# One matmul for two key branches: shared scores in the second attention of a hybrid decoder layer, with its scaling moved forward and its dense work paced lower

## The chip, the cores and the metric

The kernel runs on one core of a Trainium2 chip. The metric is the device time of one execution in microseconds. TensorE (PE) multiplies, VectorE (DVE), ScalarE (ACT) and GpSimd (POOL) do the elementwise work, and SyncE (SP) issues the loads.

## The reference

One decoder layer over 512 tokens of width 1024, in float32. A normed input is projected into the columns of four token mixers; their outputs, each multiplied by a SiLU gate path, are projected, gated and added up. Two mixers are attentions of 8 heads of 64:

```python
y_a = fox_attention(rms_norm(heads(qa, FOX_HEADS), qn_a), rms_norm(heads(ka, FOX_HEADS), kn_a),
                    heads(va, FOX_HEADS), fa + b_forget)          # first attention, with decay
...
y_c = nsa_attention(rms_norm(heads(qc, NSA_HEADS), qn_c), ...)    # second attention
# in it, for each block of 128 queries:
k_sel = ks_blk[b_ix, g_ix, top_idx]                               # "selected" keys, branch s
s_s = jnp.einsum('bqgrd,bgqkld->bgrqkl', q_i, k_sel) * scale
s_w = jnp.einsum('bqgrd,bkgd->bgrqk', q_i, k_wi) * scale          # "window" keys, branch w
return g[:, :, 0] * o_c + g[:, :, 1] * o_s + g[:, :, 2] * o_w     # and compressed keys, o_c
```

With 512 tokens the selection of 16 blocks of 64 takes all 8 blocks that there are and the window covers all 512 positions, so branches s and w are both causal attentions of the same queries, over different keys and values.

## The kernel before

Every float32 matrix is split into a high part and a rest (`h`, `l` in names), and products are sums of matmuls over the parts. **Dense work** is the projections `z_...`: blocks of 24 matmuls of 128x512 (`zgen`, `chunks`), whose weights are loaded (`r_...`), and split by ScalarE or GpSimd (high) and VectorE (rest) into `w_...`.

**Attention** goes by units (class `Unit`): in the first a head is a unit (`a0` to `a7`), in the second a head is two units (`s0`, `w0`, and so on to `w7`). For a unit `scores` runs over the four blocks of 128 queries, from 3 down to 0: block i has (i + 1) x 128 causal keys. Two matmuls (`ka`, `kb`: parts of the keys) go to one of two score banks `s_...`; VectorE reads the bank with the mask and writes probabilities' arguments `p_...` with a row extreme into `nm_...`; ScalarE takes the exponential; after block 0 GpSimd scales the rows (`p_...<-p_...,nm_...`). `finish` then transposes the probabilities through banks `tb`, splits them into `ph` and `pl`, and multiplies with the values (`o_...`). `attend` writes the scores of the next unit ahead of `finish` of the one before.

`fill(us)` writes that much dense work between attention steps. Its amount per step is `G` = 0.68 us times a pace, `FOX` for the first attention and `NSA` for the second. Generators in `side` advance with dense steps.

`nsa_scales` finishes the norm of the second attention's queries `zq_c` and keys `zkm`: small VectorE steps on `tsc`, then eight GpSimd multiplies. It is called between the attentions. `k_operand` and `q_operand` then transpose and split keys (`kt_...`) and queries (`qt_...`).

Order: from the first projections to the end of the second attention the writing order is only a priority. A planner (class `Order`) records instructions with what they need, and a list scheduler with assumed costs picks for each engine the earliest written one that is ready. Behind the second attention come the recurrence's gates (`g`), merges and the output, from which later instructions may be drawn ahead.

Of the kernel before, what the change touches and what calls it, by code (L numbers as in the profile page):

```python
# [10 lines left out]
F32 = mybir.dt.float32  # L11
# [6 lines left out]
P = 128  # L18
# [48 lines left out]
class Order:  # L67
# [72 lines left out]
    def plan(self):  # L140
# [106 lines left out]
def tile_hybrid_layer(ctx: ExitStack, tc: tile.TileContext, x, xT, units, small, bsp, out):  # L247
# [9 lines left out]
    def behind(op):  # L257
        return order.behind(op) if order.on else tc.issue_after(op)
# [299 lines left out]
    ssa = cp.tile([P, 4, 16], F32, name="ssa")  # L558
    tsa = cp.tile([P, 2, 64], F32, name="tsa")
# [123 lines left out]
    xbt = pool("xbp", xbs).tile([P, 4, S], F32, name="xb")  # L683
# [22 lines left out]
    def k_operand(z, c0, gcol, kt, name):  # L706
        ka, kb = kt
        t_ = heads(z, c0, "kt_" + name)
        g = cc[:, gcol:gcol + 1]
        for e in range(2):  # L710
            r, o = HALF[e], HALF[1 - e]
            ACT.activation(ka[r, e, :], t_[r, :], AF.Identity, scale=g[r, :])
            DVE.scalar_tensor_tensor(kb[r, e, :], t_[r, :], g[r, :], f32(ka[r, e, :]), op0=ALU.mult, op1=ALU.subtract)
            POOL.tensor_scalar(ka[o, e, :], f32(ka[r, e, :]), 1.0, 0.0, op0=ALU.mult, op1=ALU.add)

    def k_tiles(pl_, name):
        ka = pl_.tile([P, 2, S], F32R, name="ka_" + name)
        kb = pl_.tile([P, 2, S], F32R, name="kb_" + name)
        for e in range(2):
            POOL.memset(f32(kb[HALF[1 - e], e, :]), 0.0)  # L720
# [12 lines left out]
    def scores(u, gap):
        u.p = p = ap.tile([P, 1280], F32, tag="p", bufs=2, name="p_" + u.name)
        nm = ap.tile([P, 12], F32, tag="nm", bufs=4, name="nm_" + u.name)
        for i in (3, 2, 1, 0):
            n = (i + 1) * P
            s = sbank(f"s_{u.name}{i}")
            qs = u.q[:, i * P:(i + 1) * P]
            PE.matmul(s[:, :n], lhsT=qs, rhs=u.ka[:, :n], start=True, stop=False)  # L740
            PE.matmul(s[:, :n], lhsT=u.q2[:, i * P:(i + 1) * P], rhs=u.kb[:, :n], start=False, stop=True)
            pi = p[:, OFF[i]:OFF[i] + n]
            DVE.tensor_tensor_reduce(out=pi, in0=s[:, :n], in1=maskm[:, 384 - i * P:512], scale=-1.0, scalar=BIG,
                                     op0=ALU.add, op1=ALU.min, accum_out=nm[:, i:i + 1])
            ACT.activation(pi, pi, AF.Exp, scale=-1.0, bias=nm[:, i:i + 1], accum_out=nm[:, 4 + i:5 + i])
            fill(gap)
        r = nm[:, 8:12]
        DVE.reciprocal(r, nm[:, 4:8])
        if u.gate is not None:
            DVE.tensor_tensor(r, r, u.gate, op=ALU.mult)  # L750
        for i in range(4):
            pi = p[:, OFF[i]:OFF[i] + (i + 1) * P]
            POOL.tensor_scalar(pi, pi, nm[:, 8 + i:9 + i], 0.0, op0=ALU.mult, op1=ALU.add)
# [4 lines left out]
    def transposes(u, g_):  # L758
# [4 lines left out]
        for c, (j, i) in enumerate(PIECES[g_]):  # L763
            PE.transpose(t_[:, c * P:(c + 1) * P], u.p[:, OFF[i] + j * P:OFF[i] + (j + 1) * P], identf)
# [84 lines left out]
    nb = kts[0][1][0:40, 1, :]  # L849
    ACT.copy(nb[0:8, :], negc)  # L850
    DVE.tensor_tensor(nb[32:40, :], negc, f32(nb[0:8, :]), op=ALU.subtract)
    ACT.copy(kts[0][1][64:104, 0, :], f32(nb))
    for e, o in ((0, 64), (1, 0)):
        POOL.tensor_scalar(kts[1][1][o:o + 40, e, :], f32(nb), 1.0, 0.0, op0=ALU.mult, op1=ALU.add)
    later(*chunks("kv", xh, xl, emit_kv), *chunks("qc", xh, xl, emit_z(zq_c, ssc, 4, 8, ap)),
# [22 lines left out]
    def fox_units():  # L878
# [8 lines left out]
        for i in range(4):  # L887
            kt, q = kts[i % 2], nxt[i]
            for e in range(2):
# [42 lines left out]
    NSA = 1.1  # L932
    FOX = 1.2
# [182 lines left out]
    kts = [k_tiles(rp2, nm) for nm in "sw"]  # L1116
    nsa_scales()
# [13 lines left out]
    k_operand(zk_c, 0, KNC, kts[0], "s")  # L1131
# [4 lines left out]
    ws = []  # L1136

# [30 lines left out]
    def second_keys():  # L1168
        k_operand(zk_c, P, KNC, kts[1], "w")
        fill(4 * G)  # L1170

    def nsa_units():
        q = q0
        for i in range(4):
# [3 lines left out]
            for n in range(4):  # L1178
                e, b = n // 2, n % 2
                h = i + 4 * e  # L1180
                if n == 1:
                    while not ready:
# [3 lines left out]
                ka, kb = kts[b]  # L1186
                yield Unit(f"{'sw'[b]}{h}", q[:, e, :], ka[:, e, :], kb[:, e, :], v_c, 2 * b + e,
                           gate=gates[:, :, 8 * (b + 1) + h], first=b == 0, last=b == 1,
                           acc=add_cmp(cell, e) if b else None, then=second_keys if i == n == 0 else None,
                           done=lambda o, h=h: evict(o, y["c"][:, h // 2, :], h % 2, f"c{h}"))  # L1190
# [572 lines left out]
```

## Time and profile before

| | |
|---|---|
| median of 3 runs | 712.65 us (712.14 to 713.6) |
| profiled execution | 713.0 us, of which the span is 711.3 |
| busy | PE 98%, DVE 80%, ACT 51%, POOL 24% |
| matmuls | 3357 |
| first attention | about 78 to 201 us from the span's start |
| second attention | about 223 to 382 us |

A row of single instructions gives its start, its duration, the engine, the operation, out<-in and shape, and in brackets the idle time before it with what ended that. A matmul's duration runs from its start to its modelled end, and the next one starts well before that: the distance from start to start is what a matmul costs. Rows of stages give the stretch, and for each engine busy time and instructions.

### The profile page before, as it was taken

How to read it: one execution, taken by the hardware profiler on the slowest of the kernel's cores; microseconds unless marked ns; L12 is line 12 of the kernel's file. 1: busy time of each engine (PE TensorE's matmuls, PEld its weight loads, DVE VectorE, ACT ScalarE, POOL GpSimd, SP SyncE). 2: the span in 40 equal slices, each digit the busy share in tenths (PEclk: the TensorE clock that was granted, in tenths of full speed). 3: DMA queues.
4: the chain of work that ended last, by engine and by line, in shares of the span. 5: the costliest groups of instructions: out<-in, count | busy, mean ns of one | idle time of the engine just before them, and what ended most of it. 6: DMA issues, size and time to landing. Idle time of an engine off the chain costs nothing.

```text
span 711.3 us, 9561 instructions
## 1 busy us (share of the span) xinstructions
PE 700.0 (98%) x3357; PEld 573.4 (81%) x3357; DVE 571.0 (80%) x1090; ACT 362.3 (51%) x677; POOL 171.2 (24%) x230
## 2 busy tenths in 40 slices
PE   8999999999999999999999999999999999999997
PEld 6888778887877888888777888888888888888876
DVE  5799676677389949889897879999778858958995
ACT  4552555675524237776566881434534551653641
POOL 4124652453346303333244312100000000000000
PEclk9999999999999999999999999999999999999999
DMA  8613132111113431100201232333522333133302
GB/s 312 240 59 119 39 110 90 60 60 62 58 60 127 141 118 60 59 31 4 87 29 60 83 110 80 102 126 138 178 93 85 113 125 112 36 119 119 118 30 88
DMA packets 20640, 68.35 MB, mean 96 GB/s; under 512 B 2416, under 2 KB 2800, under 8 KB 20592
## 3 DMA queue, kind: packets, MB, share of 16 engines
q1 hardware_dynamic: 20160, 67.25, 28.4%
q8 instruction: 26, 0.43, 0.2%
q10 hardware_dynamic: 432, 0.49, 0.2%
q14 instruction: 22, 0.18, 0.1%
HBM read 65.64 MB, written 2.10 MB: 95 GB/s over the span
## 4 chain that ended last, share of the span: by engine, by line
PE 78%; DVE 13%; issue 3%; ACT 3%; DMA 2%; POOL 2%; SPq 0%; DVEq 0%; POOLq 0%; ACTq 0%
PE pj L223 9%; PE z_mg L223 6%; PE tb L211 3%; PE z_qc L211 3%; PE z_ud L211 3%; PE z_gb L223 3%; PE z_qa L211 3%; PE z_va L211 3%; PE o_s L211 3%; PE mg2y L223 2%; PE z_vd L211 2%; PE mg1y L223 2%; PE z_xb L211 2%; PE z_ka L211 2%; PE z_kv L211 2%
## 5 line engine op out<-in xcount | busy, mean ns | idle before, releaser
L223 PE MATMUL pj<-w_wb,yh 128*128 128x512 f32 x256 | 79.8, 389 | 0.0
L223 PEld LDWEIGHTS pj<-w_wb,yh 128*128 128x128 f32 x256 | 48.1, 188 | 9.9
L223 PE MATMUL pj<-w_wb,yl 128*128 128x512 f32 x128 | 49.8, 389 | 0.0
L223 DVE TENSOR_TENSOR w_wb<-r_wb,w_wb 128x512 fp32r<-128x512 f32 x32 | 20.9, 686 | 9.5 <-ACT w_wb L223 8.5
L223 PEld LDWEIGHTS pj<-w_wb,yl 128*128 128x128 f32 x128 | 24.0, 188 | 4.9
L211 POOL TENSOR_SCALAR p_w<-p_w,nm_w 128x128 f32<-128x128 f32 (+3 forms) x32 | 16.8, 543 | 39.2 <-DVE nm_w L211 39.2
L211 DVE TENSOR_TENSOR pl_a<-tb,ph_a 128x512 fp32r<-128x512 f32 (+1 forms) x24 | 14.4, 598 | 14.2 <-ACT ph_a L211 14.0
L211 ACT CAST ph_a<-tb 128x512 fp32r<-128x512 f32 (+1 forms) x24 | 12.4, 517 | 23.3 <-PE tb L211 23.1
L211 PE MATMUL z_xb<-xh,w_xb 128*128 128x512 f32 x64 | 24.0, 409 | 0.0
L211 ACT ACTIVATE p_s<-p_s,nm_s 128x512 f32<-128x512 f32 (+3 forms) x32 | 17.8, 559 | 11.8 <-DVE nm_s L211 11.1
L211 PE MATMUL z_gd<-xh,w_gd 128*128 128x512 f32 x64 | 22.7, 403 | 0.9 <-DVE w_gd L211 0.8
L211 ACT ACTIVATE p_w<-p_w,nm_w 128x512 f32<-128x512 f32 (+3 forms) x32 | 17.9, 561 | 10.2 <-DVE nm_w L211 10.1
L211 POOL TENSOR_SCALAR p_a<-p_a,nm_a 128x128 f32<-128x128 f32 (+3 forms) x32 | 19.7, 633 | 12.7 <-DVE nm_a L211 12.0
L211 PE MATMUL z_ud<-xh,w_ud 128*128 128x512 f32 x64 | 22.6, 400 | 0.0
L211 POOL TENSOR_SCALAR p_s<-p_s,nm_s 128x128 f32<-128x128 f32 (+3 forms) x32 | 17.3, 560 | 21.3 <-ACT ph_w L211 8.0
L211 ACT ACTIVATE p_a<-p_a,nm_a 128x512 f32<-128x512 f32 (+3 forms) x32 | 17.9, 560 | 7.0 <-DVE nm_a L211 6.9
L211 PE MATMUL z_ga<-xh,w_ga 128*128 128x512 f32 x64 | 21.3, 398 | 0.0
L211 DVE CUSTOM_DVE_ANT_0 p_a<-s_a,maskm 128x512 f32<-128x512 f32 (+3 forms) x32 | 15.3, 486 | 7.4 <-PE s_a L211 4.0
L223 PE MATMUL z_gb<-xh,w_gb 128*128 128x512 f32 x64 | 21.1, 390 | 0.0
L223 ACT CAST w_wb<-r_wb 128x1024 fp32r<-128x1024 f32 x12 | 12.6, 1047 | 15.5 <-issue 15.5
L211 DVE CUSTOM_DVE_ANT_0 p_s<-s_s,maskm 128x512 f32<-128x512 f32 (+3 forms) x32 | 15.0, 485 | 4.3 <-PE s_s L211 3.8
L211 DVE TENSOR_TENSOR pl_w<-tb,ph_w 128x512 fp32r<-128x512 f32 (+1 forms) x24 | 14.0, 598 | 3.0 <-ACT ph_w L211 2.8
(812 smaller groups left out, 2323.8 us busy)
## 6 DMA issues: line engine op xcount, KB each, us to landing
r_wb<-in_units_dram SPq DMA_DIRECT2D x16, 512.0 KB, 3.7
xt<-in_x_dram SPq DMA_DIRECT2D x4, 512.0 KB, 8.4
r_ga<-in_units_dram SPq DMA_DIRECT2D x4, 512.0 KB, 3.7
r_gd<-in_units_dram SPq DMA_DIRECT2D x4, 512.0 KB, 3.9
r_ud<-in_units_dram SPq DMA_DIRECT2D x4, 512.0 KB, 4.2
r_gc<-in_units_dram SPq DMA_DIRECT2D x4, 512.0 KB, 3.7
r_xb<-in_units_dram SPq DMA_DIRECT2D x4, 512.0 KB, 3.8
r_gb<-in_units_dram SPq DMA_DIRECT2D x4, 512.0 KB, 3.8
```

Source lines behind the costliest of these rows:

```text
L211: getattr(self.eng[name], method)(*args, **kw)
L223: return lambda *args, **kw: real(*args, **kw).ins
```

## The change

1. In the second attention a head's two units are made together (`twin`). Both branches' keys lie in one tile with a branch index. For query blocks 3 and 2 each unit has its own matmuls as before. For blocks 1 and 0 the unit `s` issues one matmul whose moving operand is the keys of both branches (2 x 256 and 2 x 128 columns); VectorE and ScalarE then work on the two halves of the bank apart. The probabilities are in two tiles: `p0_...` (blocks 0 and 1, three buffers) and `p_...` (blocks 2 and 3, two). The second branch's keys are made inside the first unit (`amid`), not after it.
2. `nsa_scales` becomes a side generator, started when the last block of the `qc` projection is out, in the first attention.
3. Paces: `FOX` 1.2 to 0.6, `NSA` 1.1 to 0.5. A window unit, which has only two steps left, fills twice at each.
4. The first attention's decay operand `q2` gets four slots in a buffer that it shares with the later convolution input `xb`; two small tiles move to another pool. The planner finds the users of a buffer's former tile when it plans, no longer when it records.

```diff
-                need.update((m, True) for m, *_ in self.seen.get(self.before[t], ()))
+            for t in ops[i][6]:
+                need.update((m, True) for m, *_ in self.seen.get(self.before.get(t), ()))
...
+    q2s = xbp.tile([P, 4, S], F32R, tag="xb", bufs=1, name="q2s")
...
+    def start(u):
+        u.low = ap.tile([P, 384], F32, tag="p0", bufs=3, name="p0_" + u.name)
+        u.nm = ap.tile([P, 12], F32, tag="nm", bufs=4, name="nm_" + u.name)
...
     def scores(u, gap):
-        u.p = p = ap.tile([P, 1280], F32, tag="p", bufs=2, name="p_" + u.name)
+        both = [u, u.twin] if u.twin else [u]
+        for x in both:
+            if x.low is None:
+                start(x)
+        u.high = ap.tile([P, 896], F32, tag="p", bufs=2, name="p_" + u.name)
         for i in (3, 2, 1, 0):
-            n = (i + 1) * P
+            if i < 2 and len(both) == 1 and u.gate is not None:
+                continue
+            us = both if i < 2 else [u]
+            n, m = (i + 1) * P, (i + 1) * P * len(us)
             s = sbank(f"s_{u.name}{i}")
-            PE.matmul(s[:, :n], lhsT=qs, rhs=u.ka[:, :n], start=True, stop=False)
-            PE.matmul(s[:, :n], lhsT=u.q2[:, i * P:(i + 1) * P], rhs=u.kb[:, :n], start=False, stop=True)
+            k = (slice(None), slice(0, 2) if len(us) > 1 else u.ka[1], slice(0, n))
+            PE.matmul(s[:, :m], lhsT=u.q[:, i * P:(i + 1) * P], rhs=u.ka[0][k], start=True, stop=False)
+            PE.matmul(s[:, :m], lhsT=u.q2[:, i * P:(i + 1) * P], rhs=u.kb[0][k], start=False, stop=True)
+            for c, x in enumerate(us):
...
-            fill(gap)
+            fill(gap * (2 if u.gate is not None and len(both) == 1 else 1))
...
         rsqrt(ssc, y_, tsc[:, 1, :].rearrange("p (t h) -> p t h", t=4))
+        yield 0.0
...
+    def last_qc(t, ps):
+        emit_qc(t, ps)
+        if t == 3:
+            side.append(nsa_scales())
...
-    NSA = 1.1
-    FOX = 1.2
+    NSA = 0.5
+    FOX = 0.6
...
-    kts = [k_tiles(rp2, nm) for nm in "sw"]
-    nsa_scales()
+    kts = k_tiles(rp2, "c", 2)
```

What stands where, before and after. First TensorE at the low query blocks of the selected unit of the second pair of units (`s_s` its score bank, `tb` and `o_s` the transposes and values of the unit ahead, `z_...` dense work). Before:

```order
L211 MATMUL z_gc_2104<-xh,w_gc_2103 128x512
L211 MATMUL s_s_2017<-ka_s,q_c_1936 128x256
L211 MATMUL s_s_2017<-kb_s,q_c_1936 128x256
L211 MATMUL z_gc_2104<-xl,w_gc_2103 128x512
L211 MATMUL z_gc_2104<-xh,w_gc_2103 128x512 x2
L211 MATMUL z_gc_2104<-xl,w_gc_2103 128x512
L211 MATMUL z_gc_2104<-xh,w_gc_2103 128x512
L211 MATMUL s_s_2018<-ka_s,q_c_1936 128x128
L211 MATMUL s_s_2018<-kb_s,q_c_1936 128x128
L211 MATMUL tb_1907<-identf,p_w_1998 128x128 x2
```

After (`ka_c` and `kb_c` hold both branches):

```order
L211 MATMUL tb_79<-identf,p_w_1905 128x128 x2
L211 MATMUL z_ud_1977<-xl,w_ud_1965 128x512
L211 MATMUL s_s_1987<-ka_c,q_c_1895 128x512
L211 MATMUL s_s_1987<-kb_c,q_c_1895 128x512
L211 MATMUL s_s_1988<-ka_c,q_c_1895 128x256
L211 MATMUL s_s_1988<-kb_c,q_c_1895 128x256
L211 MATMUL z_ud_1977<-xh,w_ud_1965 128x512 x2
L211 MATMUL z_ud_1977<-xl,w_ud_1965 128x512
```

Before, blocks 1 and 0 of this unit have 256 and 128 columns, and the window unit has another such four matmuls some 30 and 40 rows on; now 512 and 256 columns serve both units, and the window unit's four are gone.

Next GpSimd at the scaling (`zkm`, `zq_c`; `p_a` are the first attention's probabilities, `ka_s` keys of the second, `w_...` weights being split). Before:

```order
L211 MEMSET kcn 64x128
L211 MEMSET hsk 64x128
L211 TENSOR_TENSOR zkm<-zkm,tsc 128x256
L211 TENSOR_TENSOR zq_c<-zq_c,tsc 128x512
L211 TENSOR_TENSOR zkm<-zkm,tsc 128x256
L211 TENSOR_TENSOR zq_c<-zq_c,tsc 128x512
L211 TENSOR_TENSOR zkm<-zkm,tsc 128x256
L211 TENSOR_TENSOR zq_c<-zq_c,tsc 128x512
L211 TENSOR_TENSOR zkm<-zkm,tsc 128x256
L211 TENSOR_TENSOR zq_c<-zq_c,tsc 128x512
L211 TENSOR_SCALAR w_gd_1955<-r_gd_1954 128x1024
L211 TENSOR_SCALAR ka_s<-ka_s 64x512 x2
```

After:

```order
L211 TENSOR_SCALAR w_vd.01_917<-r_vd.01_916 128x1024
L211 TENSOR_TENSOR zkm<-zkm,tsc 128x256
L211 TENSOR_TENSOR zq_c<-zq_c,tsc 128x512
L211 TENSOR_TENSOR zkm<-zkm,tsc 128x256
L211 TENSOR_TENSOR zq_c<-zq_c,tsc 128x512
L211 TENSOR_TENSOR zkm<-zkm,tsc 128x256
L211 TENSOR_SCALAR p_a_887<-p_a_887,nm_a_888 128x128
L211 TENSOR_SCALAR p_a_887<-p_a_887,nm_a_888 128x256
L211 TENSOR_SCALAR p_a_889<-p_a_889,nm_a_888 128x384
L211 TENSOR_SCALAR p_a_889<-p_a_889,nm_a_888 128x512
L211 TENSOR_TENSOR zq_c<-zq_c,tsc 128x512
L211 TENSOR_TENSOR zkm<-zkm,tsc 128x256
```

Before, the eight multiplies stand between the attentions, ahead of the second attention's first keys; now five stand ahead of the last head's scaling of the first attention, and three behind it.

Last TensorE where the first attention ends (`o_a` its values, `z_ga` the gate projection, `z_vd` a projection of another mixer). Before:

```order
L211 MATMUL o_a_924<-ph_a_931,v_a 128x256
L211 MATMUL o_a_924<-pl_a_932,v_a 128x256
L211 MATMUL z_ga_928<-xh,w_ga_921 128x512
L211 MATMUL z_ga_928<-xl,w_ga_921 128x512
L211 MATMUL z_ga_928<-xh,w_ga_921 128x512 x2
L211 MATMUL z_ga_928<-xl,w_ga_921 128x512
L211 MATMUL z_ga_928<-xh,w_ga_921 128x512 x2
L211 MATMUL z_ga_928<-xl,w_ga_921 128x512
L211 MATMUL z_ga_928<-xh,w_ga_921 128x512
L211 MATMUL z_ga_1930<-xh,w_ga_1929 128x512
```

After:

```order
L211 MATMUL o_a_905<-ph_a_910,v_a 128x256
L211 MATMUL z_vd_914<-w_vd.01_917,xl 128x512
L211 MATMUL o_a_905<-pl_a_911,v_a 128x256
L211 MATMUL z_vd_914<-w_vd.01_917,xh 128x512
L211 MATMUL z_vd_915<-w_vd.01_917,xh 128x512
L211 MATMUL z_vd_915<-w_vd.01_917,xl 128x512
L211 MATMUL z_vd_915<-w_vd.01_917,xh 128x512 x2
L211 MATMUL z_vd_915<-w_vd.01_917,xl 128x512
L211 MATMUL z_vd_915<-w_vd.01_917,xh 128x512
L211 MATMUL z_vd_912<-w_vd.10_920,xh 128x512
L211 MATMUL z_vd_912<-w_vd.10_920,xl 128x512
L211 MATMUL z_vd_912<-w_vd.10_920,xh 128x512 x2
```

Before, the gate projection stands there and the other projection is done; now that projection's last blocks of 48 matmuls (`w_vd.10`, `w_vd.11`) follow with nothing of an attention between them. In the same way the convolution's projection `z_xb` ended ahead of the scores of the seventh of the eight pairs of units, and now ends beside the transposes of the eighth; from the third to the sixth pair dense rows are about as few in the one order as in the other.

More of the change, by code (lines that the diff above doesn't have):

```diff
@@ L257, in behind @@
     def behind(op):
-        return order.behind(op) if order.on else tc.issue_after(op)
+        if order.on:
+            return order.behind(op)
+        return nullcontext() if isinstance(op, int) else tc.issue_after(op)
     def shut(stack):
@@ L711, in k_operand @@
             r, o = HALF[e], HALF[1 - e]
[L712 to L720, printed above, removed]
+            ACT.activation(ka[r, e, b, :], t_[r, :], AF.Identity, scale=g[r, :])
@@ new lines, in k_operand, with k_tiles @@
+            DVE.scalar_tensor_tensor(kb[r, e, b, :], t_[r, :], g[r, :], f32(ka[r, e, b, :]), op0=ALU.mult, op1=ALU.subtract)
+            POOL.tensor_scalar(ka[o, e, b, :], f32(ka[r, e, b, :]), 1.0, 0.0, op0=ALU.mult, op1=ALU.add)
+    def k_tiles(pl_, name, nb=1):
+        ka = pl_.tile([P, 2, nb, S], F32R, name="ka_" + name)
+        kb = pl_.tile([P, 2, nb, S], F32R, name="kb_" + name)
+        for b in range(nb):
+            for e in range(2):
+                POOL.memset(f32(kb[HALF[1 - e], e, b, :]), 0.0)
@@ new lines, in scores @@
+            PE.matmul(s[:, :m], lhsT=u.q[:, i * P:(i + 1) * P], rhs=u.ka[0][k], start=True, stop=False)
+            PE.matmul(s[:, :m], lhsT=u.q2[:, i * P:(i + 1) * P], rhs=u.kb[0][k], start=False, stop=True)
+            for c, x in enumerate(us):
+                pi, nm = x.row(i), x.nm
+                DVE.tensor_tensor_reduce(out=pi, in0=s[:, c * n:(c + 1) * n], in1=maskm[:, 384 - i * P:512], scale=-1.0,
+                                         scalar=BIG, op0=ALU.add, op1=ALU.min, accum_out=nm[:, i:i + 1])
+                ACT.activation(pi, pi, AF.Exp, scale=-1.0, bias=nm[:, i:i + 1], accum_out=nm[:, 4 + i:5 + i])
@@ L749, in scores @@
+            fill(gap * (2 if u.gate is not None and len(both) == 1 else 1))
+            if u.amid and i == 3:
+                u.amid()
+        r = u.nm[:, 8:12]
+        DVE.reciprocal(r, u.nm[:, 4:8])
         if u.gate is not None:
@@ L763, in transposes @@
         for c, (j, i) in enumerate(PIECES[g_]):
-            PE.transpose(t_[:, c * P:(c + 1) * P], u.p[:, OFF[i] + j * P:OFF[i] + (j + 1) * P], identf)
+            PE.transpose(t_[:, c * P:(c + 1) * P], u.row(i)[:, j * P:(j + 1) * P], identf)
         ph, pl_ = (ap.tile([P, S], F32R, tag=w, bufs=3, name=f"{w}_{u.name}{g_}") for w in ("ph", "pl"))
@@ L848, in tile_hybrid_layer @@
     kts = [k_tiles(kp, f"a{b}") for b in range(2)]
[L849 removed]
+    nb = kts[0][1][0:40, 1, 0, :]
     ACT.copy(nb[0:8, :], negc)
     DVE.tensor_tensor(nb[32:40, :], negc, f32(nb[0:8, :]), op=ALU.subtract)
[L852 removed]
+    ACT.copy(kts[0][1][64:104, 0, 0, :], f32(nb))
     for e, o in ((0, 64), (1, 0)):
[L854 to L855 removed]
+        POOL.tensor_scalar(kts[1][1][o:o + 40, e, 0, :], f32(nb), 1.0, 0.0, op0=ALU.mult, op1=ALU.add)
+    emit_qc = emit_z(zq_c, ssc, 4, 8, ap)
+    def last_qc(t, ps):
+        emit_qc(t, ps)
+        if t == 3:
+            side.append(nsa_scales())
+    later(*chunks("kv", xh, xl, emit_kv), *chunks("qc", xh, xl, last_qc),
           zgen("cm0", 0, cm_use(0)), zgen("cm0", 1, cm_use(1)))
@@ L1136, in tile_hybrid_layer @@
     ws = []
+    xbt = xbp.tile([P, 4, S], F32, tag="xb", bufs=1, name="xb")
     def conv(i, ps):
@@ L1185, in nsa_units @@
                     fill(G)
[L1186 to L1190, printed above, removed]
+                if b == 0:
+                    pair = [Unit(f"{'sw'[j]}{h}", q[:, e, :], (kts[0][:, e], j), (kts[1][:, e], j), v_c, 2 * j + e,
+                                 gate=gates[:, :, 8 * (j + 1) + h], first=j == 0, last=j == 1,
+                                 acc=add_cmp(cell, e) if j else None, amid=second_keys if i == n == j == 0 else None,
+                                 done=lambda o, h=h: evict(o, y["c"][:, h // 2, :], h % 2, f"c{h}")) for j in range(2)]
+                    pair[0].twin = pair[1]
+                yield pair[b]
                 if n == 1:
```

37 lines of the change are left out of this document (15 added, 22 removed).

## The prediction

> **What bounds the kernel now.** I read the page's busy times first, then the chain of work that ended last, then busy times by stage, then single matmuls.
>
> ```profile
> span 711.3 us, 9561 instructions
> PE 700.0 (98%) x3357; PEld 573.4 (81%) x3357; DVE 571.0 (80%) x1090; ACT 362.3 (51%) x677; POOL 171.2 (24%) x230
> PEclk9999999999999999999999999999999999999999
> PE 78%; DVE 13%; issue 3%; ACT 3%; DMA 2%; POOL 2%; SPq 0%; DVEq 0%; POOLq 0%; ACTq 0%
> 549.84 5.44 PE mg1z L223 x24
> ```
>
> TensorE is the bound: in use for 98% of the span at full granted clock, with 78% of the chain. The last row, from the chain, gives the price of a full matmul with nothing in its way: 5.44/24 = 0.227 us from start to start (128x512). Gains come from fewer matmuls, or from the time that TensorE loses between them. I call that time slack: over all matmuls of a stage, the distance from one start to the next, less the price of that shape. The other prices:
>
> ```profile
> 288.16 0.28 PE L211 MATMUL s_s<-ka_s,q_c 128*128 128x256 f32 x1
> 288.27 0.28 PE L211 MATMUL s_s<-kb_s,q_c 128*128 128x256 f32 x1
> 288.39 0.63 PE L211 MATMUL z_gc<-xh,w_gc 128*128 128x512 f32 x2
> 289.19 0.22 PE L211 MATMUL s_s<-ka_s,q_c 128*128 128x128 f32 x1
> 289.25 0.28 PE L211 MATMUL s_s<-kb_s,q_c 128*128 128x128 f32 x1
> 289.37 0.65 PE L211 MATMUL tb<-identf,p_w 128*128 128x128 f32 x4
> 309.27 0.34 PE L211 MATMUL s_w<-ka_w,q_c 128*128 128x384 f32 x1
> 309.44 0.28 PE L211 MATMUL o_s<-pl_w,v_c 128*128 128x256 f32 x1
> 229.07 0.60 PE L211 MATMUL kt_w<-identf,zkm 128*128 128x128 f32 x4
> 229.43 0.71 PE L211 MATMUL z_gd<-xh,w_gd 128*128 128x512 f32 x2
> 229.97 0.39 PE L211 MATMUL z_gd<-xl,w_gd 128*128 128x512 f32 x1
> ```
>
> By starts: a pair of 256 columns 0.23, a pair of 128 columns 0.18, one of 384 0.17; four transposes with the delay of what follows 0.90 - 2 x 0.227 = 0.45. With these (0.227, 0.175, 0.119, 0.085, and 0.109 a transpose) I summed the slack by stage, for the matmuls counted in the PE column:
>
> ```profile
> core 0: us, PE busy (x) PEld busy (x) DVE busy (x) ACT busy (x) POOL busy (x), PEclk, DMA share, GB/s
> 84.00:200.00 116.00, 115.27 (x590) 95.60 (x590) 78.41 (x165) 66.42 (x147) 49.50 (x72) 1.00 0.23 73
> 200.00:226.00 26.00, 24.31 (x112) 18.54 (x111) 23.88 (x42) 7.36 (x11) 16.97 (x17) 1.00 0.31 101
> 226.00:262.00 36.00, 35.82 (x178) 29.39 (x178) 25.85 (x72) 13.22 (x32) 7.51 (x10) 1.00 0.41 132
> 262.00:383.00 121.00, 120.04 (x689) 100.01 (x688) 104.53 (x301) 79.57 (x210) 42.21 (x70) 1.00 0.15 49
> 383.00:395.00 12.00, 11.83 (x51) 8.95 (x50) 11.97 (x17) 8.83 (x14) 5.26 (x6) 1.00 0.26 79
> ```
>
> Slack: first attention (84 to 200) 3.9 us; change of attention (200 to 226) 3.6; compression (226 to 262) 0.9; second attention (262 to 383) 9.1; recurrence gates (383 to 395) 0.9. Together 18.4 us is all that reordering can win; most of it never shows as idle, since a matmul's bar of 0.39 us covers the start of the next. VectorE is busy 92% of 200 to 226 and 86% of 262 to 383, so it is the engine that TensorE waits for there.
>
> **The change, part by part.**
>
> *Shared scores.* A pair of units (selected and window keys of one head) issues 16 score matmuls now, 12 after: blocks 1 and 0 cost 2 x (0.23 + 0.18) = 0.82 us now, and after it a pair of 512 and a pair of 256, 0.45 + 0.23 = 0.68. Eight pairs x 0.14 = 1.1 us, all on the bounding engine. VectorE's and ScalarE's rows per unit stay (mask, exponential), so they win nothing. New waits: two mask reads now hold one score bank, so the next score waits for both. At worst that is the second read, 8 x 0.42 us = 3.4 (the 256-column read below); at best below nothing, as bank hand-overs fall from 8 to 6 per pair. I take 0, being nearer to the hand-over end: dense matmuls stand beside each pair in the new order.
>
> ```profile
> 228.52 0.42 DVE L211 CUSTOM_DVE_ANT_0 p_s<-s_s,maskm 128x256 f32<-128x256 f32 x1
> ```
>
> By the Trainium skill (TensorE: Matmul & The Clock Gate, "Back-to-back issue gap"), an isolated warm matmul takes N/2.4 + 2.5 ns; by that estimate a pair would win only 0.01 us and all eight 0.1. The trace disagrees: its second 128-column matmul holds the next for 0.12 us, not 0.056.
>
> *Scaling forward.* Now eight GpSimd multiplies stand between the attentions:
>
> ```profile
> 209.49 2.06 POOL L211 TENSOR_TENSOR zkm<-zkm,tsc 128x256 f32<-128x256 f32 x1 [6.50 <-DVE tsc L211]
> 218.64 1.49 POOL L211 TENSOR_TENSOR zq_c<-zq_c,tsc 128x512 f32<-128x512 f32 x1
> 210.40 0.68 DVE L211 TENSOR_TENSOR w_gd<-r_gd,w_gd 128x512 fp32r<-128x512 f32 x1
> 211.60 1.50 DVE L211 TENSOR_TENSOR w_gd<-r_gd,w_gd 128x512 fp32r<-128x512 f32 x1
> 214.04 2.06 DVE L211 TENSOR_TENSOR w_w1k<-r_w1k,w_w1k 128x1024 fp32r<-128x1024 f32 x1
> 227.38 1.22 DVE L211 TENSOR_TENSOR w_w1k<-r_w1k,w_w1k 128x1024 fp32r<-128x1024 f32 x1
> 223.56 0.47 PE L211 MATMUL s_s<-ka_s,q_c 128*128 128x512 f32 x1 [0.67 <-DVE q_c L211]
> 225.71 0.73 PE L211 MATMUL z_gd<-xh,w_gd 128*128 128x512 f32 x2 [0.77 <-DVE w_gd L211]
> ```
>
> They run from 209.5 to 220.1 and hold up the keys' transposes; beside them VectorE's own work stretches (0.68 to 1.50, 1.22 to 2.06), and the two last rows are TensorE paying. After, the multiplies stand in the last two heads of the first attention, where VectorE is 68% busy (78.4 of 116). In the new order 48 full matmuls of the last projection follow that attention with nothing of it between: 48 x 0.227 = 10.9 us of cover while VectorE prepares keys and weights. So the 4.5 us of slack from 200 to 262 should fall to the rate of the first attention, 3.9/116 = 0.034 us per us, over 62 us 2.1: a gain of 2.4. It can be as little as the 1.4 us of the two waits and as much as 4.5.
> What it costs: five of the multiplies stand on GpSimd ahead of the last head's probability scaling (some 7 us at 1.4 each), and the split of a projection weight stands behind the other three. Late next would be the last head's transposes; the dense matmuls of that projection cover them. The multiplies will stretch VectorE there as they do here; the two stretches shown sum to 1.7 us. I book 0.3, between none and 1.7. By the Trainium skill (GPSIMD Engine Reference, "1. Specifications") GpSimd shares its SBUF interfaces with VectorE instructions that have two SBUF inputs, which speaks against putting these multiplies beside an attention; the trace agrees in the rows above.
>
> *Lower pace.* The dense matmuls and their number stay; they are only written later, and the planner lets a ready attention step go first. First attention: 3.9 us of slack; I take 0.5 off, since its late waits (the row below) come where the attention chain lies behind dense work. Second attention: by the two orders its last projection ended ahead of the last two pairs and now reaches the eighth, but in the middle the dense rows are as thin in both. Its 9.1 us (0.075 per us) at the 0.034 of the first attention would be 4.1; I take a fifth of that 5.0, 1.0. The ends are -7.7 (the slack rate of 200 to 226, worked out with the rivals) and 5.0; I stay near what stands there now, since VectorE's share does. The gates get dense matmuls ahead of them: 0.4 of 0.9, none to all.
>
> ```profile
> 163.70 0.66 PE L211 MATMUL tb<-identf,p_a 128*128 128x128 f32 x4 [0.59 <-DVE pl_a L211]
> ```
>
> *The rest* costs nothing: the keys in one tile have the same four clears; four slots for the decay operand instead of two only take a wait from GpSimd (24% busy); the buffer that this operand shares with the convolution is free when the first attention ends, and the convolution comes in the second; loads are the same 142, in a slightly other order.
>
> **Sum**: 1.1 + 2.4 - 0.3 + 0.5 + 1.0 + 0.4 = 5.1 us. The profiled execution took 713.0 (711.3 and 1.7 around it), which lies 0.35 above the median of 712.65: 713.0 - 5.1 = 707.9, or 707.5 on the median's scale.
>
> **The rivals.** *Waits re-form*: TensorE wins the 1.1 us and each other wait comes back elsewhere, since VectorE's work is unchanged. For it: VectorE at 86%. Against it: the waits sit where VectorE is at 92%, and its work there is spread over more matmuls. 713.0 - 1.1 - 0.35 = 711.5.
> *Bigger gain*: half of all slack goes, 9.2 + 1.1, for which the first attention's rate speaks: 702.4.
> *Slower*: with attention first and fewer dense matmuls between, VectorE becomes the bound in the second attention. Its price is the slack rate of 200 to 226, 3.6/26 = 0.14 us per us, over 121 us 16.8 instead of 9.1: 7.7 lost instead of 1.0 won, 707.5 + 8.7 = 716.2. It decides once VectorE's share there goes from 86% to 92%, some 7 us of work or stretching. Against it: the same VectorE rows, and about as many matmuls to cover them.
>
> **How the numbers follow.** A difference within 0.2% (711.2 to 714.1) can't be told from no change. Forecast 0.66 (faster); bigger gain 0.12 (faster); waits re-form 0.14 (same); slower 0.08. So faster 0.78, same 0.14, slower 0.08. Time 707.5. The range runs from 703.4 (the forecast with the full 4.5, half of the 5.0 and all 0.9 of the gates won) to 712.0, which takes in the re-formed waits and leaves out bigger gain and slower, 2 in 10.
>
> **What would show it.** 32 matmuls fewer; no GpSimd multiplies or waits for `q_c` and `w_gd` in the change of attention; `zkm` scaled before the first attention ends; VectorE's share of the second attention still under 90%; the slack of 200 to 262 halved. It is wrong if TensorE's starts in the second attention spread out, or if the last heads of the first attention wait for probabilities.

## The result, and the profile after

The changed kernel took 705.04 us (median of 4 runs, 704.66 to 706.73); the kernel before, run beside it, 712.74. The ratio is 0.9896, 95% interval 0.9876 to 0.9915: 7.7 us faster. The forecast was 707.5 with a range of 703.4 to 712.0. Direction and range held, but 5.1 us of gain were forecast and 7.7 came.

The page of the changed kernel, its span, busy times and shares of the chain that ended last:

```profile
span 703.6 us, 9505 instructions
PE 694.7 (99%) x3325; PEld 573.5 (82%) x3325; DVE 568.2 (81%) x1090; ACT 357.0 (51%) x675; POOL 166.6 (24%) x230
PE 81%; DVE 11%; ACT 5%; issue 1%; DMA 1%; POOL 0%; SPq 0%; DVEq 0%; ACTq 0%; POOLq 0%
```

TensorE has 32 matmuls fewer (3357 before). The other engines run as many instructions as before to within two, and are busy 3 to 5 us less each (VectorE 571.0 to 568.2, ScalarE 362.3 to 357.0, GpSimd 171.2 to 166.6). VectorE's part of the chain fell from 13% to 11%.

For busy times by stage I now cut both kernels at the same work, not at the same times: the first attention from 84 us to its last output matmul, the change up to the first score of the second attention, the compression up to the first window score (`s_w`), the second attention up to its last output matmul, and the gates. First the kernel before, then the changed one:

```profile
84.04:201.07 117.03, 116.22 (x594) 96.25 (x592) 78.85 (x168) 66.79 (x148) 49.46 (x72) 1.00 0.22 73
201.07:223.56 22.49, 21.74 (x100) 17.02 (x101) 21.03 (x39) 6.99 (x10) 15.22 (x15) 1.00 0.35 115
223.56:265.88 42.32, 41.28 (x204) 33.57 (x205) 30.59 (x82) 14.22 (x36) 9.27 (x13) 1.00 0.39 126
265.88:381.73 115.85, 114.89 (x660) 95.60 (x659) 101.94 (x292) 77.73 (x203) 41.42 (x69) 1.00 0.14 46
381.73:394.68 12.95, 12.78 (x55) 9.76 (x54) 11.88 (x16) 9.62 (x15) 6.05 (x6) 1.00 0.22 65
```

```profile
84.08:178.71 94.63, 94.55 (x502) 79.36 (x501) 75.02 (x170) 59.73 (x138) 46.60 (x66) 1.00 0.23 75
178.71:201.13 22.42, 22.42 (x104) 18.55 (x103) 19.21 (x40) 10.74 (x16) 9.60 (x17) 1.00 0.35 111
201.13:254.26 53.13, 52.79 (x260) 43.21 (x259) 32.41 (x75) 16.39 (x42) 12.83 (x16) 1.00 0.34 109
254.26:367.91 113.65, 113.19 (x637) 94.86 (x636) 102.04 (x292) 76.67 (x201) 41.92 (x68) 1.00 0.15 48
367.91:384.59 16.68, 16.68 (x76) 13.83 (x75) 15.68 (x20) 9.30 (x15) 7.16 (x7) 1.00 0.28 89
```

The first attention has some 90 matmuls fewer in it: dense ones, which now stand behind it, most of them in the compression and the gates. VectorE's busy time in the second attention is the same (101.9 and 102.0 us), and so its share rises from 88% to 90% in the shorter stage. TensorE nevertheless loses less there. With the prices of the prediction, and 0.09 us for matmuls of 64 columns, which it left out, the slack (start to start, less the price of the shape) of each stage in us:

| stage | before | after | gain | forecast |
|---|---|---|---|---|
| ahead of 84 us | 6.67 | 7.17 | -0.5 | 0 |
| first attention | 4.25 | 2.73 | 1.5 | 0.5 - 0.3 |
| change and compression | 4.25 | 1.65 | 2.6 | 2.4 |
| second attention | 8.81 | 5.96 | 2.9 | 1.0 |
| gates | 1.02 | -0.01 | 1.0 | 0.4 |
| after the gates | 2.39 | 3.17 | -0.8 | 0 |
| 32 matmuls, by price | | | 1.0 | 1.1 |
| sum | | | 7.7 | 5.1 |

TensorE's waits of the changed kernel, by what they waited for (us in total, times, longest):

```profile
PE warm L223 <- DVE warm L223: 1.5, 1, 1.5
PE z_mg L223 <- DVE acc L223: 0.8, 1, 0.8
PE z_ka L211 <- POOL w_ka.00_144 L211: 0.5, 1, 0.5
PE z_kv L211 <- DVE v_a L211: 0.5, 1, 0.5
PE z_gd L211 <- DVE sgd L211: 0.3, 1, 0.3
...
PE tb L211 <- DVE pl_w L211: 0.3, 1, 0.3
```

The waits for `q_c` (0.67 before) and `w_gd` (0.77) are gone, as forecast. The second row is new, 0.8 us in the merge ahead of `mg2`. On GpSimd the multiplies stand where the order had them, in the first attention, and take 0.61 to 1.71 us each instead of up to 2.06:

```profile
159.12 0.61 POOL L211 TENSOR_TENSOR zkm<-zkm,tsc 128x256 f32<-128x256 f32 x1
...
163.76 2.05 POOL L211 TENSOR_SCALAR p_a<-p_a,nm_a 128x128 f32<-128x128 f32 x4
165.78 1.71 POOL L211 TENSOR_TENSOR zq_c<-zq_c,tsc 128x512 f32<-128x512 f32 x1
...
168.48 1.04 POOL L211 TENSOR_TENSOR zq_c<-zq_c,tsc 128x512 f32<-128x512 f32 x1
```

### The profile page after: what moved, and what is told of

It is laid out like the page before. It is cut to its first block, busy times and chain, and to the rows that moved or that the text cites. A ratio compares the mean times of both kernels' runs of the same rounds, so it can differ in the third digit from the quotient of the medians.

```text
span 703.6 us, 9505 instructions
## 1 busy us (share of the span) xinstructions
PE 694.7 (99%) x3325; PEld 573.5 (82%) x3325; DVE 568.2 (81%) x1090; ACT 357.0 (51%) x675; POOL 166.6 (24%) x230
## 4 chain that ended last, share of the span: by engine, by line
PE 81%; DVE 11%; ACT 5%; issue 1%; DMA 1%; POOL 0%; SPq 0%; DVEq 0%; ACTq 0%; POOLq 0%
PE pj L223 10%; PE z_ka L211 3%; PE tb L211 3%; PE z_mg L223 3%; PE z_qc L211 3%; PE z_ud L211 3%; PE z_vd L211 3%; PE z_ga L211 3%; PE z_gd L211 3%; PE z_qa L211 3%; PE z_va L211 3%; PE z_xb L211 3%; PE z_gb L223 3%; PE o_s L211 2%; PE mg2y L223 2%; PE mg3y L223 2%
## 5 line engine op out<-in xcount | busy, mean ns | idle before, releaser
L223 PE MATMUL pj<-w_wb,yh 128*128 128x512 f32 x256 | 79.8, 389 | 0.0
L223 PEld LDWEIGHTS pj<-w_wb,yh 128*128 128x128 f32 x256 | 48.1, 188 | 9.9
L223 PE MATMUL pj<-w_wb,yl 128*128 128x512 f32 x128 | 49.8, 389 | 0.0
L223 DVE TENSOR_TENSOR w_wb<-r_wb,w_wb 128x512 fp32r<-128x512 f32 x32 | 20.9, 686 | 11.0 <-ACT w_wb L223 8.5
L223 PEld LDWEIGHTS pj<-w_wb,yl 128*128 128x128 f32 x128 | 24.0, 188 | 5.0
L211 ACT CAST ph_a<-tb 128x512 fp32r<-128x512 f32 (+1 forms) x24 | 12.4, 517 | 20.6 <-PE tb L211 18.3
L211 ACT ACTIVATE p_w<-p_w,nm_w 128x256 f32<-128x256 f32 (+3 forms) x32 | 17.8, 556 | 8.2 <-DVE nm_w L211 8.1
L223 PE MATMUL z_gb<-xh,w_gb 128*128 128x512 f32 x64 | 21.1, 391 | 0.0
L211 POOL TENSOR_SCALAR p_a<-p_a,nm_a 128x128 f32<-128x128 f32 (+3 forms) x32 | 18.2, 587 | 11.9 <-DVE nm_a L211 11.8
L223 ACT CAST w_wb<-r_wb 128x1024 fp32r<-128x1024 f32 x12 | 12.6, 1048 | 15.5 <-issue 15.5
L223 ACT ACTIVATE tm<-z_mg 128x512 f32<-128x512 f32 x8 | 4.7, 591 | 25.7 <-PE z_mg L223 25.7
```

Of the source, the lines that this page charges most:

```text
L211: getattr(self.eng[name], method)(*args, **kw)
L223: return lambda *args, **kw: real(*args, **kw).ins
```

## The experiments

The question was where the 2.6 us more came from. Theory P: the lower pace is worth more than the 1.9 us forecast, in the second attention above all. Theory H: the shared scores save more than their matmuls (fewer hand-overs of a score bank, an earlier start). Theory O: every edit makes the planner write a new order, and single collisions come and go with it. After the second batch theory C is added, which names the collisions.

All runs, with the gain over the kernel before on the same chip, and slack by stage (us). The 95% intervals of the ratios reach 0.13 to 0.2% to each side, 0.9 to 1.4 us; two runs of one batch are compared more closely, by their own ranges. Slack is that of the one traced execution.

| run | time | gain | first att. | change, compr. | second att. | gates |
|---|---|---|---|---|---|---|
| changed kernel | 705.04 | 7.7 | 2.73 | 1.65 | 5.96 | -0.01 |
| `e1_old_paces` | 708.34 | 4.8 | 3.43 | 0.78 | 9.76 | 0.89 |
| `e3_unshared` | 709.53 | 3.6 | 2.83 | 1.79 | 9.71 | 0.01 |
| `e4_scales_back` | 706.59 | 6.5 | 2.77 | 3.53 | 6.00 | 0.00 |
| `e2_before_low` | 709.77 | 3.3 | 2.86 | 3.18 | 7.08 | 0.29 |
| `e5_same_bank` | 707.61 | 5.3 | 2.80 | 1.85 | 7.53 | 0.07 |
| `e6_two_banks` | 708.06 | 4.8 | 2.84 | 10.1 with the next | | 0.01 |
| `e1_old_nsa` | 707.17 | 5.7 | 2.79 | 1.63 | 8.07 | 0.87 |
| `e1_old_fox` | 708.75 | 4.1 | 3.30 | 0.78 | 8.03 | 1.15 |
| `e7_old_paces_cast` | 707.72 | 5.4 | 3.36 | 0.78 | 8.69 | 0.89 |
| `e8_after_cast` | 705.30 | 7.8 | 2.81 | 1.70 | 6.66 | 0.02 |
| `e9_unshared_cast` | 706.19 | 6.9 | 2.84 | 1.79 | 6.36 | 0.30 |
| `e10_lower_cast` | 708.15 | 5.0 | 4.57 | 3.46 | 4.59 | 0.56 |

(In `e6_two_banks` the first window score comes during the compression, so the two stages can't be cut apart.)

### First batch: one part of the change at a time

Both paces back, in the changed kernel:

```diff
-    NSA = 0.5
-    FOX = 0.6
+    NSA = 1.1
+    FOX = 1.2
```

> The changed kernel with both paces back at their old values (second attention 0.5 to 1.1, first attention 0.6 to 1.2); shared scores and early scaling stay. The changed kernel took 705.0, the one before 712.7. Slack (starts of matmuls less the price of their shape) fell by 2.9 us in the second attention, 1.5 in the first and 1.0 in the gates. Theory P, the lower pace did these: 705.0 + 5.4 = 710.4, slack of the second attention back near 8.8. Theory H, the second attention's 2.9 come from the shared scores (fewer hand-overs of score banks): 705.0 + 2.5 = 707.5, its slack near 6.0. Theory O, the planner makes a new order of every edit and the gains are the luck of one order: anything from 704 to 709, and no stage goes back to its old slack.

Every unit with its own scores, in the changed kernel:

```diff
-                    pair[0].twin = pair[1]
...
-            if i < 2 and len(both) == 1 and u.gate is not None:
-                continue
...
-            fill(gap * (2 if u.gate is not None and len(both) == 1 else 1))
+            fill(gap)
```

> The changed kernel with every unit computing its own scores again (32 more score matmuls, keys still in one tile); low paces and early scaling stay. Theory P: only the matmuls' own 1.0 to 1.1 us come back, 706.1, slack of the second attention near 6.0. Theory H: also its 2.9 of slack, 708.9, slack near 8.8. Theory O: 704 to 709.

The scaling between the attentions again, in the changed kernel:

```diff
-        if t == 3:
-            side.append(nsa_scales())
...
     kts = k_tiles(rp2, "c", 2)
+    for _ in nsa_scales():
+        pass
```

> The changed kernel with the GpSimd multiplies between the attentions again; shared scores and low paces stay. Theory P with the forecast's reading (scaling forward brought the 2.6 us between the first attention and the second attention's window branch): 707.6, waits for the query keys and the weight halves of some 1.4 us back. Rival: the low pace leaves enough dense matmuls there to cover the multiplies, 705.0 to 705.5, slack of that stretch still under 2.

The paces alone, in the kernel before:

```diff
-    NSA = 1.1
-    FOX = 1.2
+    NSA = 0.5
+    FOX = 0.6
```

> The kernel before with the two paces lowered (1.1 to 0.5, 1.2 to 0.6) and nothing else. Theory P: 712.7 - 5.4 = 707.3, slack of the second attention near 6, of the first near 2.7. Theory H: at most first attention and gates, 712.7 - 2.5 = 710.2. If low pace needs the early scaling (multiplies still between the attentions, with a ready attention ahead of dense work): 711 to 713.

None of the four came out as one theory alone had it. With old paces the second attention's slack was back (9.76, P says 8.8), but the loss was 3.0 us (7.70 - 4.75) and not 5.4: the first attention gave back 0.7 of its 1.5, and the change and the compression did even better (0.78). Without sharing the same slack was back too (9.71), at low paces: H's number. Both theories cannot own the same 2.9 us. And the pace alone, in the kernel before, won 3.3 us, with 7.08 in the second attention. Scaling between the attentions cost 1.2 us by the gains (6.5 against 7.7) and 1.7 by the spans of the two profiled executions (705.3 and 703.6): between the forecast's reading (2.6) and its rival (0 to 0.5), with 3.53 of slack in that stretch where the rival had under 2. What came back was not a wait for the query keys but one behind VectorE's later work:

```profile
PE z_gd L211 <- DVE sgd L211: 1.2, 1, 1.2
```

### Second batch: what in the sharing, and which pace

In the changed kernel, two pairs of matmuls into one bank:

```diff
-            k = (slice(None), slice(0, 2) if len(us) > 1 else u.ka[1], slice(0, n))
-            PE.matmul(s[:, :m], lhsT=u.q[:, i * P:(i + 1) * P], rhs=u.ka[0][k], start=True, stop=False)
-            PE.matmul(s[:, :m], lhsT=u.q2[:, i * P:(i + 1) * P], rhs=u.kb[0][k], start=False, stop=True)
+            for c, x in enumerate(us):
+                k = (slice(None), x.ka[1], slice(0, n))
+                PE.matmul(s[:, c * n:(c + 1) * n], lhsT=u.q[:, i * P:(i + 1) * P], rhs=u.ka[0][k], start=True, stop=False)
+                PE.matmul(s[:, c * n:(c + 1) * n], lhsT=u.q2[:, i * P:(i + 1) * P], rhs=u.kb[0][k], start=False, stop=True)
```

> The changed kernel, but the shared score of a block is written by two pairs of matmuls (one pair for each branch) into the same bank: the order, the six bank hand-overs of a pair of heads' units and the early mask reads of the window unit stay; only 32 matmuls more are issued. With every unit alone the time was 709.5, the changed kernel's 705.0. If the 4.5 us between them are the early start of the window unit's two small blocks, or the fewer hand-overs: 706.1 (their own 1.0 to 1.1 us), slack of the second attention near 6. If they hang on the number of score matmuls: 709, slack near 9.7.

And with a bank for each branch, its mask read and exponential directly behind its matmuls:

```diff
-            s = sbank(f"s_{u.name}{i}")
...
+            for c, x in enumerate(us):
+                s = sbank(f"s_{x.name}{i}")
+                k = (slice(None), x.ka[1], slice(0, n))
```

> As the run before, but each branch's score has a bank of its own: eight hand-overs of a bank again (seven of eight have their own two matmuls), the window unit's two small blocks still early. Early start alone explains the gain: 706.1, slack near 6. Hand-overs explain it: 709.5, slack near 9.7. Both: between, near 708.

One pace at a time back, in the changed kernel:

```diff
-    NSA = 0.5
+    NSA = 1.1
```

> The changed kernel with the pace of the second attention alone back at 1.1. Both paces back gave 708.3, slack of the second attention 9.8. If the second attention's own pace does it: 708, slack near 9.8, first attention's slack stays near 2.7. If it is the first attention's pace (which sets how many dense matmuls are left for later): 705, slack near 6. If the order of the planner is luck: no relation, 705 to 709.

```diff
-    FOX = 0.6
+    FOX = 1.2
```

> The changed kernel with the pace of the first attention alone back at 1.2. If the second attention's own pace does it: 705.5 to 706, first attention's slack near 3.4, the second's near 6. If the first attention's pace does it: 708, the second's near 9.8. Luck: no relation, 705 to 709.

By the gains, the steps from no sharing to sharing are 1.2 us (early start), 0.5 (fewer hand-overs) and 2.4 (fewer matmuls). The middle one is not clear of noise: the ranges of its two runs overlap (707.3 to 708.2 and 707.5 to 709.1). The last is 2.4 us for matmuls priced at 1.0, which no theory had. The paces, undone one by one, cost 2.0 and 3.6 us, together 3.0: not a sum of two causes. (The five runs of `e1_old_fox` spread from 707.4 to 709.5, and the traced one took 707.4; by that one it is 2.2.) Both point to O, so the next question is which single distances between matmuls make the second attention's slack. In four of the slower versions (`e1_old_paces`, `e3_unshared`, `e6_two_banks`, `e1_old_fox`) one stretch of 15 us holds 2.7 to 3.8 us of it, with a single distance in it that is 0.8 to 1.8 us over its price; in the changed kernel no such stretch holds over 1.6. The kernel before has no such distance either: its worst 15 us hold 2.3, and no single distance in that attention is more than 0.5 over its price. With old paces, GpSimd and then TensorE:

```profile
359.37 1.05 POOL L223 TENSOR_SCALAR w_mg00.01_4003<-r_mg00.01_4001 128x1024 fp32r<-128x1024 f32 x1 [3.94 <-PE z_gc L223]
360.39 2.82 POOL L211 TENSOR_SCALAR p_w<-p_w,nm_w 128x128 f32<-128x128 f32 x4
362.60 0.33 PE L211 MATMUL tb<-identf,p_w 128*128 128x128 f32 x1 [1.54 <-POOL p_w L211]
```

GpSimd had been idle for 3.94 us; then the rounding copy of a dense weight (1.05 us) began just ahead of the scaling of a head's probabilities, and TensorE waited 1.54 us for that. The factors of that scaling (`nm_w`) had been written at 358.02, so it stood behind the copy in GpSimd's order. Without sharing, GpSimd, VectorE and TensorE:

```profile
350.51 1.06 POOL L223 TENSOR_SCALAR w_gc<-r_gc 128x1024 fp32r<-128x1024 f32 x1
351.60 0.69 DVE L223 TENSOR_TENSOR w_gc<-r_gc,w_gc 128x512 fp32r<-128x512 f32 x1 [0.95 <-POOL w_gc L223]
352.78 0.69 DVE L211 CUSTOM_DVE_ANT_0 p_s<-s_s,maskm 128x512 f32<-128x512 f32 x1
353.53 0.39 PE L211 MATMUL s_s<-ka_c,q_c 128*128 128x256 f32 x1 [1.21 <-DVE nm_s L211]
```

VectorE's queue stood 0.95 us behind the same kind of copy on GpSimd, with the mask read of the next scores behind it, and TensorE waited 1.21 us for the score bank. With the first attention's pace back, GpSimd, VectorE, GpSimd and TensorE:

```profile
364.83 1.06 POOL L223 TENSOR_SCALAR w_mg00.01_4003<-r_mg00.01_4001 128x1024 fp32r<-128x1024 f32 x1 [4.45 <-PE z_gc L223]
364.89 1.02 DVE L211 TENSOR_TENSOR nm_w<-nm_w,gates 128x4 f32<-128x4 f32 x1
366.07 3.00 POOL L211 TENSOR_SCALAR p_w<-p_w,nm_w 128x128 f32<-128x128 f32 x4 [0.18 <-DVE nm_w L211]
367.90 1.00 PE L211 MATMUL tb<-identf,p_w 128*128 128x128 f32 x4 [1.07 <-POOL p_w L211]
```

Here the copy met VectorE: the small row that makes the factors took 1.02 us beside it (0.13 with both paces back), and the scaling began when that was done. Theory C: these copies account for what both the paces and the sharing seemed to be worth beyond their price.

### Third batch: four copies moved off GpSimd

From the place in the second attention's code on where the last projections (`gc`, `xb`) are put in the queue, behind the fourth head, the rounding copies of the dense weights go to ScalarE up to the end of that attention's code (otherwise every third does):

```diff
     def hi_cast(dst, src):
         cnt["hi"] += 1
-        if cnt["act"] and cnt["hi"] % cnt["act"] == 0:
+        if "late" in cnt or cnt["act"] and cnt["hi"] % cnt["act"] == 0:
             ACT.copy(dst, src)
...
             if i == 1:
+                cnt["late"] = 1
                 later(*silu("gc", y["c"], (0, 2)), ...
```

> The run with both paces back (708.3, slack of the second attention 9.8), and the rounding copies of the projection weights from the second attention's third head on moved from GpSimd to ScalarE. In that run one copy of 1.05 us stands on GpSimd just ahead of the last head's probability scaling, and TensorE then waits 1.5 us at the transposes. Theory C (a few such collisions of weight copies with the attention make up most of what the paces seemed to be worth in the second attention): 706 or less, slack near 7.5, and no wait for p_w over 0.5. Theory P (the lower pace wins by the spread of dense matmuls itself): 708, slack near 9.8, another wait takes its place.

> The changed kernel (705.0, slack of the second attention 6.0, no wait there over 0.44) with the same copies on ScalarE. Theory C: no collision there to remove, 704.5 to 705.5. If GpSimd's copies cost it by stretching VectorE: down to 703.5. If ScalarE, 66% busy there, becomes late with its exponentials: 706 to 707.

> The run with every unit's own scores (709.5, slack 9.7) with the same copies on ScalarE. There VectorE stood 0.95 us behind a copy on GpSimd and TensorE then waited 1.2 us for a score bank. Theory C: 707 to 707.5, slack near 7.5, so that sharing is worth 2 to 2.5 us without the collisions. If sharing itself is worth the 4.5 us: 709.5, slack near 9.7.

The edit reaches less than theory C needs. It moves four copies, one of `gc` and three of `xb`, which stood on GpSimd between 262 and 327 us. The copies in the rows above (L223 in them) are written behind the second attention and drawn ahead, so the edit leaves them on GpSimd. With both paces back and the four copies moved, and then without sharing and the four copies moved:

```profile
358.15 2.07 POOL L211 TENSOR_SCALAR p_w<-p_w,nm_w 128x128 f32<-128x128 f32 x4 [2.76 <-DVE cm L211]
360.19 1.05 POOL L223 TENSOR_SCALAR w_mg00.01_4003<-r_mg00.01_4001 128x1024 fp32r<-128x1024 f32 x1
```

```profile
348.03 1.05 POOL L223 TENSOR_SCALAR w_gc<-r_gc 128x1024 fp32r<-128x1024 f32 x1 [7.88 <-DVE nm_w L211]
349.06 2.49 POOL L211 TENSOR_SCALAR p_w<-p_w,nm_w 128x128 f32<-128x128 f32 x4
```

In the first the copy now comes behind the scaling. In the second it comes 2.5 us earlier and stands just ahead of a scaling, which is the pattern blamed above, and TensorE does not wait for that scaling. The waits of 1.54 and 1.21 us are gone all the same. So these runs are the same parts in other orders, which is what theory O speaks of; what the named copies cost as such, theory C, they do not test.

The clearest result is `e9_unshared_cast` against `e8_after_cast`, on one chip: 706.19 (706.11 to 706.32) and 705.30 (704.99 to 705.49). In this pair of orders sharing is worth 0.9 us, its matmuls' price, and the second attention's slack is 6.36 and 6.66. So H falls as a property of sharing: the 4.1 us between `e3_unshared` and the changed kernel (3.6 and 7.7 of gain) were 0.9 for the matmuls and some 3 for what one order has and the other has not. Of these 3 the rows above name the wait of 1.21; the rest lies in single distances of under 0.8 us, whose causes were not traced. ScalarE's 3 us of added work in that stage made no wait for it over 0.2 us (0.2 without it too), and VectorE's stayed (second attention, without and with the four copies on ScalarE, each with every unit's own scores):

```profile
253.11:371.79 118.68, 116.00 (x670) 97.46 (x669) 102.76 (x296) 78.90 (x205) 42.05 (x68) 1.00 0.15 48
253.16:369.40 116.24, 115.14 (x674) 98.21 (x672) 103.31 (x296) 81.93 (x209) 37.47 (x64) 1.00 0.15 47
```

For the changed kernel itself the time stayed (gain 7.8 and 7.7). In the traces its second attention has 0.7 us more of slack with the copies moved (5.96 and 6.66) and the stretch ahead of 84 us, where the code is the same, 0.65 less, so a small loss there is possible. At old paces the new order gave 0.6 us (708.3 to 707.7), the slack fell from 9.76 to 8.69 where C said 7.5, and another wait for `p_w` of 0.9 us stood elsewhere, as P had said. Between `e7_old_paces_cast` and `e8_after_cast`, on one chip, the two paces are worth 2.4 us: 2.0 in the second attention, 0.9 in the gates, 0.55 in the first attention, less 0.9 in change and compression and small terms. Beyond that one wait, what makes up the 2.0 was not traced.

### Last run: lower still

```diff
-    NSA = 0.5
-    FOX = 0.6
+    NSA = 0.3
+    FOX = 0.4
```

> The changed kernel with the copies on ScalarE and both paces lower still (second attention 0.5 to 0.3, first 0.6 to 0.4). At the paces of the change this took 705.3, at the old paces 707.7, so 2.4 us lie between the two. If the gain goes on in proportion (another third of the way from 1.1 and 1.2): 704.5, slack of the second attention near 6. If the planner's order is already set by readiness and not by the pace: 705.0 to 705.6. If dense matmuls now run short in the middle of the second attention: 706 to 707, slack 8 or more.

Both paces lower still cost 2.8 us against `e8_after_cast` (gains 5.0 and 7.8), by none of the three ways: the second attention went on improving (4.59), but the first attention lost 1.8 (why was not traced) and the change with the compression 1.8. At the change the keys were now late:

```profile
PE s_s L211 <- DVE kb_c L211: 1.4, 1, 1.4
```

```profile
205.77 2.13 DVE L211 TENSOR_TENSOR w_ga<-r_ga,w_ga 128x512 fp32r<-128x512 f32 x2
207.83 0.73 DVE L211 SCALAR_TENSOR_TENSOR kb_c<-kt_w,cc,ka_c 64x512 fp32r<-64x512 f32 x1
...
209.31 0.76 DVE L211 SCALAR_TENSOR_TENSOR kb_c<-kt_w,cc,ka_c 64x512 fp32r<-64x512 f32 x1 [0.68 <-ACT ka_c L211]
210.22 0.47 PE L211 MATMUL s_s<-ka_c,q_c 128*128 128x512 f32 x1 [1.45 <-DVE kb_c L211]
```

The split of a dense weight that was put off (`w_ga`, 2.13 us on VectorE) stood ahead of the first half of the key operand, and the second half followed that. So the gain of a lower pace has an end within a third of the step made here. No run was faster than the changed kernel by more than the scatter.

## Why the prediction was right, and where it was mis-sized

*Shared scores, 1.1 us.* Right: 1.0 by the prices, 0.9 in the pair `e9_unshared_cast` and `e8_after_cast`; in the orders of `e3_unshared` and the changed kernel it was 4.1. The cost of 0 for the second mask read also held (its worst case, 8 x 0.42, counted one second read in a pair of units, and there are two, of 256 and of 128 columns): the distances ahead of the matmuls of `s_s` had 0.75 us of slack from the first score to the last output with sharing, and 0.82 before. By the rule of the Trainium skill (TensorE: Matmul & The Clock Gate, "Back-to-back issue gap") for an isolated matmul, all eight pairs would win only 0.1. The pair of runs disagrees, as the trace of before did; the same section says that the rule under-counts short matmuls in a stream.

*Scaling forward, 2.4.* The stretch gained 2.6, but the number is an average of two cases that I had not told apart. At low paces the early scaling alone brings the slack of change and compression from 3.53 (`e4_scales_back`) to 1.65, 1.9 us. At old paces early scaling and sharing together bring it from 4.25 (kernel before) to 0.78 (`e1_old_paces`), 3.5 us; the scaling alone was not run there. The lower pace by itself brings a little there when the scaling is late (4.25 to 3.18 in `e2_before_low`) and takes 0.9 away when it is early. The cover named, the 48 matmuls behind the first attention, held: the change has 0.09 us of slack.

*The 0.3 us booked beside the first attention* did not show. That attention's slack is 2.73 with the multiplies in it and 2.77 without (`e4_scales_back`).

*Lower pace, 0.5 + 1.0 + 0.4.* This is the term that was mis-sized, most of all its 1.0 for the second attention, where 2.9 came (paces and sharing together). The pace of both attentions is worth 2.4 us (`e7_old_paces_cast` to `e8_after_cast`), 3.0 (`e1_old_paces` to the changed kernel) or 3.3 (alone in the kernel before), where 1.9 was forecast. First attention: 0.55 to 0.7 where both kernels scale early (0.5 forecast), and 1.4 alone in the kernel before (4.25 to 2.86). Gates: 0.7 to 1.0, where I took 0.4 of it. Second attention: I took a fifth of 5.0 because VectorE's share would stay, and it nearly did; but the slack did not follow that share. At 90% it was 5.96, at 88% 8.81. By the runs the paces alone win 1.7 us of slack there in the kernel before (8.81 to 7.08), 2.0 with the four copies moved (8.69 to 6.66) and 3.8 in the changed kernel (9.76 to 5.96). So the pace does most of the 2.9, and the spread between these three goes with the order. The kernel before had no collision of the size shown above to lose: the longest wait of its transposes for a scaling there is 0.33 us. Why a lower pace wins in the small distances stays open.

*Not foreseen*: 0.8 us of wait in the merge (`z_mg` for `acc`). It stands in every version with the second attention's pace at 0.5 or less and in none at 1.1, so it goes with that pace: dense work put off until after the attention meets VectorE's recurrence, whose scans stand ahead of `acc` there. The whole stretch behind the gates lost less than 0.8 by it: with the changed kernel's other parts and a pace of 1.1 its slack is 2.71 to 3.05 (`e1_old_paces`, `e7_old_paces_cast`, `e1_old_nsa`; the last two have another wait of 0.4 there), in the changed kernel 3.17. The 0.5 us ahead of 84 us are not the change's: versions with the same code there lie between 6.0 and 7.2.

*The rivals.* Waits re-form: refuted by 7.7 us where it had 1.1, and by the `q_c` and `w_gd` rows that are gone. Slower, by VectorE as the bound: its share came to 90%, short of the 92% named, and its busy time stayed. Bigger gain (702.4): the result, 705.0, lies midway between it and the forecast. Its mechanism came nearer than the time says: in the stages that the prediction summed, 8.0 of 18.3 us went, nearly the half that it named, and 1.3 came back outside them.

*Left open*: why the first attention's slack fell from 4.25 to 3.43 with old paces and the rest of the change; whether the 1.2 and 0.5 us that early start and fewer hand-overs seemed to bring (`e6_two_banks`, `e5_same_bank`) are more than the order, since these two were run in one order only; and what the named copies cost, since no run moved them.

## What to carry to other kernels

When an engine's slack is spread over hundreds of small distances, an edit's price (matmuls saved times their duration) is sound, but what comes on top depends on the order that the planner makes of it: undo the same part in two orders before calling the extra a property of the edit (sharing: 4.1 us in one pair of orders, 0.9 in another). One thing to look for is an off-path copy, such as a weight's rounding, that begins just ahead of work on the path on the same engine. When an edit is meant to take such a copy away, look in the new trace whether that very copy has moved. Writing dense work later helps up to a point; past it the preparation that was put off stands in front of the next stage's operands.

## What the runs showed of the hardware that I had not expected

How much GpSimd slows beside VectorE. The same four instructions that scale one head's probabilities, with what VectorE does beside them; first without sharing, then with the scaling moved back:

```profile
348.47 2.08 POOL L211 TENSOR_SCALAR p_w<-p_w,nm_w 128x128 f32<-128x128 f32 x4 [9.07 <-DVE nm_w L211]
348.22 1.05 DVE L211 TENSOR_TENSOR pl_s<-tb,ph_s 128x512 fp32r<-128x512 f32 x2
349.90 0.75 DVE L211 SCALAR_TENSOR_TENSOR xb<-z_xb,cc,xb 128x511 f32<-128x511 f32 x1 [0.63 <-ACT xb L211]
```

```profile
217.32 4.59 POOL L211 TENSOR_SCALAR p_s<-p_s,nm_s 128x128 f32<-128x128 f32 x4 [4.81 <-DVE nm_s L211]
```

```profile
217.03 1.22 DVE L211 TENSOR_TENSOR w_w1k<-r_w1k,w_w1k 128x1024 fp32r<-128x1024 f32 x1
218.17 1.29 DVE L211 TENSOR_TENSOR w_gd<-r_gd,w_gd 128x512 fp32r<-128x512 f32 x2
```

4.59 us instead of 2.08, while VectorE's own split of a weight runs at 1.22 and 0.65 us apiece. VectorE worked beside the fast one too, but there one input of each row is a bank that TensorE wrote (`tb`, `z_xb`). In the changed kernel's first attention the same rows took 2.05. By the Trainium skill (GPSIMD Engine Reference, "1. Specifications") GpSimd shares its SBUF interfaces with VectorE instructions that have two SBUF inputs. The rows agree, and show that here GpSimd paid and not VectorE. In the rows of `e1_old_fox` above it was VectorE that paid: 1.02 us for a row that takes 0.13.

Moving four copies of 1.05 us from GpSimd to ScalarE (41.9 to 38.4 us and 76.7 to 80.9 in the second attention of the changed kernel) left the time as it was (705.0 and 705.3), although ScalarE was the busier of the two.
